# Weight splits of a transformer trunk: all high parts on ScalarE, fewer low parts on GpSimd

## The chip, the cores and the metric

The kernel runs on one core of a Trainium2 chip. The metric is device time in microseconds (us) of one execution, as the median of three runs. The engines of the core are TensorE (matmuls, PE in the profile, with its weight loads as PEld), VectorE (DVE), ScalarE (ACT), GpSimd (POOL) and SyncE (SP, which here issues most DMAs).

## The reference, cut to what matters

The program computes two layers (DEPTH = 2) of a diffusion trunk over 256 latent tokens and 256 context tokens of width 1024, in float32. Layer 0 works on both kinds of token (512 columns), layer 1 produces only the latent tokens (256 columns), though its keys and values also read the context. Each layer has two halves:

```python
m, mc = mixer_block(modulate(x, sh1, sc1), modulate(xc, sh1c, sc1c), with_ctx, ...)
x = layer_norm(ALPHA * x + g1 * m, ln1_g[l], ln1_b[l])
f = conv_ffn(modulate(x, sh2, sc2), ffn_w1[l], ffn_b1[l], ffn_conv_w[l], ffn_conv_b[l], ffn_w2[l], ffn_b2[l])
x = layer_norm(ALPHA * x + g2 * f, ln2_g[l], ln2_b[l])
```

The mixer has four branches on one input projection: a recurrent branch (a short convolution, gates, and a linear scan in both directions), differential attention, grouped-query attention with rotary embedding, and neighbourhood attention. The four results are multiplied by their branch weights, gated by `sigmoid` of 4096 further columns of the input projection, added, and projected. The feed-forward is

```python
u = dwconv(h @ w1 + b1, conv_w, conv_b, FFN_CONV // 2)
val, gate = jnp.split(u, 2, axis=-1)
return (jax.nn.silu(gate) * val) @ w2 + b2
```

with 2 x 2816 columns in `w1` and a depthwise convolution of three taps along the tokens.

## The kernel before, in words

Every large product is made from float32 operands split in two: a high part, which is the operand rounded to the type that TensorE takes at its faster rate, and a low part, the operand minus its high part. `mm3` (line 223) then adds three matmuls: high by high (line 225), and the two mixed products (lines 226 and 227). So each weight that arrives by DMA has to be split on the chip before it can be used.

Weights arrive in tiles of 1 MB named `raw` (two buffers; `raw`, line 160, issued on SyncE). Each holds two blocks of 128 x 1024 elements: a block is 128 columns of an input projection with its 8 slices of the contraction, or half of a token-major one, or a row of a second projection. `split` (line 188) turns one block into the tiles `wh` and `wl`, which are rings of four buffers each, so a block can be split while up to three earlier ones are waiting or in use. A few blocks go to tiles kept for longer (`wo`, and `w` for rows of the feed-forward's second projection), some in halves. `split` is reached from `cols_fm`, `cols_tm` and `rows`, and is called 271 times in one execution.

Which engine makes each part is decided by the running number of the split and the table `POOL` (line 105), by layer and phase. Phase 0 is the recurrent branch with its gates, 1 differential attention, 2 grouped-query attention, 3 neighbourhood attention with the merge and output projection, 4 the feed-forward with its second projection. An entry has four numbers: where the running number modulo the first is the second, GpSimd makes the high part, else ScalarE; where it is modulo the third the fourth, GpSimd makes the low part, else VectorE. The two decisions are independent, so that one block can have both parts on GpSimd.

The other work of these engines around the splits: in the feed-forward (`ffn`, line 1247), each block's result in PSUM is moved out by ScalarE twice (line 1268 into `up` with bias, line 1272 into `cv` scaled by the middle tap), VectorE adds the two outer taps (line 1275), ScalarE applies SiLU (line 1278), GpSimd multiplies the two halves (line 1279), and the product is split by ScalarE and VectorE (lines 804 and 805 in `hilo`). GpSimd also clears the border columns of `up` (lines 1266 and 1267). A pair of blocks of the value half and one of the gate half make one turn of the loop over `pair`, which has 11 turns in each layer. PSUM has three buffers for these results. In the recurrent branch (`lru`, line 686) VectorE runs the scans (lines 771 to 776) while TensorE works on the gate columns of that branch (`gates`, line 615). In attention, VectorE takes the row maxima (line 845) and ScalarE the exponentials (line 846).

The order of the instructions on each engine is not the order of the program text: `TileContext(nc, schedule_with_timeline_sim=True)` orders them at build time by a simulated timeline, within the program's data dependencies, a few hand-written ones (`hold`, `issue_after`) and the buffers of each tag. On the chip each engine then runs its list in that order.

Of the kernel before, what the change touches and what calls it, by code (L numbers as in the profile page):

```python
# [12 lines left out]
ALU = mybir.AluOpType  # L13
# [88 lines left out]

POOL = (((4, 0, 8, 2), (4, 0, 8, 2), (4, 0, 8, 0), (5, 2, 8, 2), (6, 5, 8, 2)), ((4, 0, 4, 1), (4, 0, 4, 2), (4, 0, 100, 6), (4, 0, 4, 2), (2, 0, 4, 0)))


LATE = ((8, 8, 4, 8), (8, 8, 4, 8))
# [2 lines left out]
class Trunk:  # L111
# [76 lines left out]
    def split(self, src, hi, lo):  # L188

        nc = self.nc  # L190
        self.n_split += 1
        ph, po, lp, lo_at = POOL[self.l][self.phase]
        if self.n_split % ph == po:
            nc.gpsimd.tensor_scalar(out=hi, in0=src, scalar1=1.0, scalar2=0.0, op0=ALU.mult, op1=ALU.add)  # L194
        else:
            nc.scalar.copy(hi, src)  # L196
        eng = nc.gpsimd if self.n_split % lp == lo_at else nc.vector
        eng.tensor_tensor(out=lo, in0=src, in1=hi.bitcast(F32), op=ALU.subtract)  # L198
        return hi, lo

# [1302 lines left out]
```

## Time and profile before

| | before |
|---|---|
| median of 3 runs | 1532.49 us (1530.24 to 1534.35) |
| profiled execution | 1532.55 us |
| its span | 1530.8 us |
| TensorE busy | 1421.7 us (93%) |
| TensorE weight loads busy | 1173.0 us (77%) |
| VectorE busy | 968.4 us (63%) |
| ScalarE busy | 640.8 us (42%) |
| GpSimd busy | 505.5 us (33%) |
| mean HBM traffic | 137 GB/s |

The span is the time from the first to the last recorded instruction; the execution's own time is a little longer. Shares of busy time are means over stages. The stages, in us from the start of the span: layer 0's mixer to about 500, its output stage to 560, its feed-forward to 818 and second projection to 935, layer 1's mixer from 960 to 1265, its output stage to 1318, its feed-forward to 1464, its second projection and the end to 1531. TensorE's matmuls are pipelined and their ends are modelled, so a busy TensorE is not necessarily at its peak; the starts of consecutive matmuls tell its rate.

### The profile page before, as it was taken

How to read it: one execution, taken by the hardware profiler on the slowest of the kernel's cores; microseconds unless marked ns; L12 is line 12 of the kernel's file. 1: busy time of each engine (PE TensorE's matmuls, PEld its weight loads, DVE VectorE, ACT ScalarE, POOL GpSimd, SP SyncE). 2: the span in 40 equal slices, each digit the busy share in tenths (PEclk: the TensorE clock that was granted, in tenths of full speed). 3: DMA queues.
4: the chain of work that ended last, by engine and by line, in shares of the span. 5: the costliest groups of instructions: out<-in, count | busy, mean ns of one | idle time of the engine just before them, and what ended most of it. 6: DMA issues, size and time to landing. Idle time of an engine off the chain costs nothing.

```text
span 1530.8 us, 22339 instructions
## 1 busy us (share of the span) xinstructions
PE 1421.7 (93%) x8420; PEld 1173.0 (77%) x8420; DVE 968.4 (63%) x1692; ACT 640.8 (42%) x1137; POOL 505.5 (33%) x612
## 2 busy tenths in 40 slices
PE   5989999899999989999999999988889997899987
PEld 3757767777877768777778887888688985798976
DVE  4674665743534987555554428775776558799965
ACT  3452353153254345444444124572525254455522
POOL 2241001421433523222222402250122545466662
PEclk9999999999999999999999999998899999899999
DMA  9336612223524354444444432434423546355562
GB/s 344 129 110 188 201 56 86 88 83 96 172 93 155 106 194 141 165 146 159 166 138 137 152 138 74 154 114 124 163 87 112 147 143 199 132 166 165 166 222 109
DMA packets 149022, 218.90 MB, mean 143 GB/s; under 512 B 9990, under 2 KB 118882, under 8 KB 148914
## 3 DMA queue, kind: packets, MB, share of 16 engines
q1 hardware_dynamic: 146402, 212.74, 42.0%
q0 software_dynamic: 2512, 4.73, 1.2%
q8 instruction: 67, 1.10, 0.3%
q14 instruction: 41, 0.34, 0.1%
HBM read 208.23 MB, written 1.08 MB: 137 GB/s over the span
## 4 chain that ended last, share of the span: by engine, by line
PE 65%; DVE 15%; issue 6%; DMA 5%; ACT 5%; POOL 2%; SPq 2%; DVEq 0%; ACTq 0%; POOLq 0%
PE mm L225 15%; PE mm L226 14%; PE mm L227 14%; DVE wl L198 4%; PE acc L227 3%; PE acc L226 3%; PE acc L225 3%; DVE cv L1275 3%; PE ops L869 3%; PE adaps L362 2%; ACT wh L196 2%; DMA raw<-in_w_in_dram 2%; PE tp L861 2%; DMA raw<-in_ffn_w_dram 1%; POOL cv L1279 1%
## 5 line engine op out<-in xcount | busy, mean ns | idle before, releaser
L225 PE MATMUL mm<-hh,wh 128*128 128x256 f32 (+1 forms) x1488 | 505.0, 342 | 17.9 <-POOL wh L194 5.3
L227 PE MATMUL mm<-hh,wl 128*128 128x256 f32 (+1 forms) x1488 | 498.7, 336 | 2.3 <-DVE wl L198 1.3
L226 PE MATMUL mm<-hl,wh 128*128 128x256 f32 (+1 forms) x1488 | 499.0, 336 | 0.5 <-DVE hl L344 0.5
L198 DVE TENSOR_TENSOR wl<-raw,wh 128x1024 fp32r<-128x1024 f32 x212 | 284.1, 1346 | 171.4 <-ACT wh L196 134.3
L225 PEld LDWEIGHTS mm<-hh,wh 128*128 128x128 f32 x1488 | 285.3, 193 | 63.9 <-issue 17.5
L196 ACT CAST wh<-raw 128x1024 fp32r<-128x1024 f32 x182 | 189.7, 1047 | 293.3 <-PE mm L226 110.0
L227 PEld LDWEIGHTS mm<-hh,wl 128*128 128x128 f32 x1488 | 285.1, 192 | 33.4 <-issue 2.5
L226 PEld LDWEIGHTS mm<-hl,wh 128*128 128x128 f32 x1488 | 285.4, 192 | 32.7 <-issue 4.0
L1275 DVE SCALAR_TENSOR_TENSOR cv<-up,par,cv 128x512 f32<-128x512 f32 (+1 forms) x176 | 157.9, 907 | 43.2 <-ACT cv L1272 30.9
L194 POOL TENSOR_SCALAR wh<-raw 128x1024 fp32r<-128x1024 f32 x73 | 89.5, 1226 | 270.4 <-PE mm L226 96.8
L198 POOL TENSOR_TENSOR wl<-raw,wh 128x1024 fp32r<-128x1024 f32 x43 | 116.3, 2706 | 117.2 <-ACT wh L196 104.9
L1279 POOL TENSOR_TENSOR cv<-cv 128x512 f32<-128x512 f32 (+1 forms) x44 | 54.2, 1232 | 155.5 <-ACT cv L1278 155.5
L226 PE MATMUL acc<-wl,a 128*128 128x512 f32 x232 | 92.3, 398 | 4.2 <-DVE wl L198 3.0
L227 PE MATMUL acc<-wh,a 128*128 128x512 f32 x232 | 92.0, 397 | 0.0
L225 PE MATMUL acc<-wh,a 128*128 128x512 f32 x232 | 91.1, 398 | 0.0
L845 DVE TENSOR_REDUCE nm<-sps 128x1 f32<-128x512 f32 (+1 forms) x96 | 56.3, 598 | 51.4 <-PE sps L890 34.6
L846 ACT ACTIVATE e<-sps,nm 128x512 f32<-128x512 f32 (+1 forms) x96 | 59.1, 618 | 64.1 <-DVE nm L845 50.5
L225 PE MATMUL mm<-wh,hh 128*128 128x256 f32 x240 | 68.6, 286 | 0.0
L227 PE MATMUL mm<-wh,hl 128*128 128x256 f32 x240 | 68.3, 284 | 0.0
L226 PE MATMUL mm<-wl,hh 128*128 128x256 f32 x240 | 67.8, 283 | 0.0
L293 ACT ACTIVATE junk<-x,nmu 128x512 bf16<-128x512 f32 x44 | 31.7, 721 | 85.3 <-DVE nmu L285 47.6
L1278 ACT ACTIVATE cv<-cv 128x512 f32<-128x512 f32 (+1 forms) x44 | 23.1, 525 | 94.1 <-DVE cv L1275 93.9
(311 smaller groups left out, 2323.6 us busy)
## 6 DMA issues: line engine op xcount, KB each, us to landing
raw<-in_ffn_w_dram SPq DMA_DIRECT2D x66, 1024.0 KB
raw<-in_w_in_dram SPq DMA_DIRECT2D x52, 1024.0 KB
raw<-in_w_ada_dram SPq DMA_DIRECT2D x40, 1024.0 KB
raw<-in_w_branch_dram SPq DMA_DIRECT2D x8, 1024.0 KB
raw<-in_w_out_dram SPq DMA_DIRECT2D x8, 1024.0 KB
w<-in_w_ada_dram SPq DMA_DIRECT2D x4, 1024.0 KB
w<-in_w_ada_dram SPq DMA_DIRECT2D x8, 512.0 KB
qk<-dp SPq DMA_DIRECT2D x48, 64.0 KB
```

What stands on the lines that cost most here:

```text
L194: nc.gpsimd.tensor_scalar(out=hi, in0=src, scalar1=1.0, scalar2=0.0, op0=ALU.mult, op1=ALU.add)
L196: nc.scalar.copy(hi, src)
L198: eng.tensor_tensor(out=lo, in0=src, in1=hi.bitcast(F32), op=ALU.subtract)
L225: nc.tensor.matmul(out, lhsT=lh, rhs=rh, start=start, stop=False)
L226: nc.tensor.matmul(out, lhsT=lh, rhs=rl, start=False, stop=False)
L227: return nc.tensor.matmul(out, lhsT=ll, rhs=rh, start=False, stop=stop)
L293: nc.scalar.activation(self.junk, halves[n], AF.Square, bias=nmu, accum_out=q[n])
L845: nc.vector.tensor_reduce(out=nm, in_=s if fold is None else fold, op=ALU.max, axis=AX.X, negate=True)
L846: nc.scalar.activation(e, s, AF.Exp, bias=nm, accum_out=total)
L869: self.last_pv = nc.tensor.matmul(o[64 * hh:64 * hh + 64, cs], lhsT=v[:, kt, vcol(hh)], rhs=pts[hh][:, kt, :], start=kt == 0, stop=kt == n ...
L1275: nc.vector.scalar_tensor_tensor(out=cv, in0=up[:, :, k:k + 256], scalar=tap[k], in1=cv, op0=ALU.mult, op1=ALU.add)
L1279: nc.gpsimd.tensor_tensor(out=conv[0], in0=conv[0], in1=conv[1], op=ALU.mult)
```

## The change

The table loses its rule for high parts, and `split` loses the branch: every high part is made by ScalarE. The rule for low parts stays as it was in phases 1 to 4 (an entry that never matched a split, in phase 2 of layer 1, is now `None`), and in phase 0 of both layers no low part is made by GpSimd. Nothing else is edited; the planner orders the new program anew.

```diff
-POOL = (((4, 0, 8, 2), (4, 0, 8, 2), (4, 0, 8, 0), (5, 2, 8, 2), (6, 5, 8, 2)), ((4, 0, 4, 1), (4, 0, 4, 2), (4, 0, 100, 6), (4, 0, 4, 2), (2, 0, 4, 0)))
+POOL = ((None, (8, 2), (8, 0), (8, 2), (8, 2)), (None, (4, 2), None, (4, 2), (4, 0)))
...
         nc = self.nc
         self.n_split += 1
-        ph, po, lp, lo_at = POOL[self.l][self.phase]
-        if self.n_split % ph == po:
-            nc.gpsimd.tensor_scalar(out=hi, in0=src, scalar1=1.0, scalar2=0.0, op0=ALU.mult, op1=ALU.add)
-        else:
-            nc.scalar.copy(hi, src)
-        eng = nc.gpsimd if self.n_split % lp == lo_at else nc.vector
+        nc.scalar.copy(hi, src)
+        turn = POOL[self.l][self.phase]
+        eng = nc.gpsimd if turn and self.n_split % turn[0] == turn[1] else nc.vector
         eng.tensor_tensor(out=lo, in0=src, in1=hi.bitcast(F32), op=ALU.subtract)
         return hi, lo
```

Counted through the program's order of splits (the counts of the page agree), by layer and phase:

| layer, phase | splits | high parts on GpSimd before | after | low parts on GpSimd before | after |
|---|---|---|---|---|---|
| 0, recurrent | 12 | 3 | 0 | 2 | 0 |
| 0, attention and merge (1 to 3) | 56 | 12 | 0 | 7 | 7 |
| 0, feed-forward and second projection | 69 | 12 | 0 | 8 | 8 |
| 1, recurrent | 14 | 3 | 0 | 3 | 0 |
| 1, attention and merge (1 to 3) | 54 | 14 | 0 | 9 | 9 |
| 1, feed-forward and second projection | 66 | 33 | 0 | 16 | 16 |
| all | 271 | 77 | 0 | 45 | 40 |

## Rows read from the trace of the kernel before

**Rows 1.** Page, costliest groups: line, engine, operation, tiles, count, then busy, mean ns, idle.
```profile
L196 ACT CAST wh<-raw 128x1024 fp32r<-128x1024 f32 x182 | 189.7, 1047 | 293.3 <-PE mm L226 110.0
...
L194 POOL TENSOR_SCALAR wh<-raw 128x1024 fp32r<-128x1024 f32 x73 | 89.5, 1226 | 270.4 <-PE mm L226 96.8
L198 POOL TENSOR_TENSOR wl<-raw,wh 128x1024 fp32r<-128x1024 f32 x43 | 116.3, 2706 | 117.2 <-ACT wh L196 104.9
```

**Rows 2.** Busy time by stretch; the last is one pair of blocks.
```profile
560.00:818.00 258.00, 254.87 (x1388) 201.36 (x1387) 150.38 (x232) 124.57 (x180) 68.09 (x148) 0.99 0.48 159
1035.00:1160.00 125.00, 109.39 (x763) 98.27 (x762) 88.63 (x194) 44.86 (x83) 22.54 (x21) 0.88 0.39 121
1160.00:1265.00 105.00, 101.02 (x788) 92.13 (x788) 55.34 (x87) 50.86 (x96) 47.37 (x49) 1.00 0.42 135
1318.00:1464.00 146.00, 138.85 (x1079) 133.42 (x1079) 133.85 (x143) 75.34 (x155) 92.23 (x141) 1.00 0.48 158
1361.60:1374.65 13.05, 12.16 (x99) 11.68 (x98) 12.18 (x13) 6.74 (x16) 8.56 (x13) 1.00 0.50 163
```

**Rows 3.** Groups of 1318 to 1464 us by form: busy, mean ns, idle before, releaser.
```profile
L1275 DVE SCALAR_TENSOR_TENSOR cv<-up,par,cv 128x256 f32<-128x256 f32 x88 | 85.6, 991 | 6.4 <-ACT cv L1272 4.8
...
L1278 ACT ACTIVATE cv<-cv 128x256 f32<-128x256 f32 x22 | 9.2, 418 | 49.9 <-DVE cv L1275 49.9
...
L194 POOL TENSOR_SCALAR wh<-raw 128x1024 fp32r<-128x1024 f32 x23 | 30.0, 1304 | 24.3 <-DMA raw<-in_ffn_w_dram 15.3 <-PE mm L226 8.1 <-PE mm L227 0.9
```

**Rows 4.** Two lines in that stretch: ns minimum/median/maximum, first and last start us.
```profile
L1275 DVE SCALAR_TENSOR_TENSOR cv<-up,par,cv x88: 471/954/2624, 1321.3 to 1463.0; 128x256 f32<-128x256 f32 x88
...
L198 DVE TENSOR_TENSOR wl<-raw,wh x34: 1209/1214/1978, 1321.7 to 1463.4; 128x1024 fp32r<-128x1024 f32 x34
```

**Rows 5.** Timeline, one pair of blocks: start us, us, engine, line, operation, idle before.
```profile
1362.39 1.05 POOL L194 TENSOR_SCALAR wh<-raw 128x1024 fp32r<-128x1024 f32 x1 [0.94 <-DMA raw<-in_ffn_w_dram]
...
1369.72 1.45 POOL L194 TENSOR_SCALAR wh<-raw 128x1024 fp32r<-128x1024 f32 x1 [0.41 <-PE mm L227]
...
1362.69 1.82 DVE L198 TENSOR_TENSOR wl<-raw,wh 128x1024 fp32r<-128x1024 f32 x1 [0.53 <-ACT wh L196]
...
1370.18 1.27 DVE L1275 SCALAR_TENSOR_TENSOR cv<-up,par,cv 128x256 f32<-128x256 f32 x1
...
1363.54 0.19 PEld L225 LDWEIGHTS mm<-hh,wh 128*128 128x128 f32 x1 [0.94 <-POOL up L1267]
...
1364.48 0.28 PE L226 MATMUL mm<-hl,wh 128*128 128x256 f32 x1
1364.60 0.28 PE L227 MATMUL mm<-hh,wl 128*128 128x256 f32 x1
```

**Rows 6.** Timeline of the recurrent branches: GpSimd low parts, and VectorE beside them.
```profile
985.80 2.50 POOL L198 TENSOR_TENSOR wl<-raw,wh 128x1024 fp32r<-128x1024 f32 x1 [1.96 <-ACT wh L196]
...
1003.39 2.41 POOL L198 TENSOR_TENSOR wl<-raw,wh 128x1024 fp32r<-128x1024 f32 x1 [0.24 <-ACT wh L196]
...
985.96 3.42 DVE L198 TENSOR_TENSOR wl<-raw,wh 128x1024 fp32r<-128x1024 f32 x1
...
1024.40 3.36 DVE L198 TENSOR_TENSOR wl<-raw,wh 128x1024 fp32r<-128x1024 f32 x1
```

**Rows 7.** Timeline around the longest TensorE wait for a GpSimd high part.
```profile
104.48 1.06 ACT L196 CAST wh<-raw 128x1024 fp32r<-128x1024 f32 x1 [3.17 <-DMA raw<-in_w_in_dram]
...
108.42 2.28 DVE L198 TENSOR_TENSOR wl<-raw,wh 128x1024 fp32r<-128x1024 f32 x1
...
109.59 2.02 POOL L194 TENSOR_SCALAR wh<-raw 128x1024 fp32r<-128x1024 f32 x1
...
111.66 0.80 PE L225 MATMUL mm<-hh,wh 128*128 128x512 f32 x1 [5.34 <-POOL wh L194]
...
112.68 0.63 PE L227 MATMUL mm<-hh,wl 128*128 128x512 f32 x1
113.11 0.63 PE L225 MATMUL mm<-hh,wh 128*128 128x512 f32 x1
```

## The prediction

> **What bounds the kernel now.** I read the page's table of engines first: TensorE is busy 93% of the span, VectorE 63%, ScalarE 42%, GpSimd 33%. Two thirds of the chain of waits is TensorE, so an edit to the weight splits is worth something only where TensorE stands still and waits for them. The second view is therefore busy time by stretch [rows 2]. In the feed-forward of layer 0 (560 to 818 us) TensorE is busy 254.87 of 258 us; nothing that happens to a split shows there. In the feed-forward of layer 1 (1318 to 1464 us), where half as many tokens pass each weight, TensorE is busy 138.85 of 146, VectorE 133.85, GpSimd 92.23 and ScalarE only 75.34. There the loop over pairs of blocks repeats every 13.05 us, with VectorE busy 12.18 of them, so VectorE sets the pace. TensorE's own need is less: consecutive 256-column matmuls start 0.12 us apart [rows 5], a pair has 4 blocks of 24, and 96 x 0.12 = 11.5 us. Its weight loads show the rest as gaps, such as the 0.94 us at 1363.54 [rows 5].
>
> The third view is durations. VectorE's convolution step takes 471 ns at best, 954 in the median and 2624 at worst, its low part 1209 at best and 1978 at worst [rows 4]. The same instruction on the same shape differs that much by what GpSimd does beside it: the low part at 1362.69 takes 1.82 us while GpSimd makes a high part from 1362.39 to 1363.44, and the convolution step at 1370.18 takes 1.27 us beside the GpSimd high part at 1369.72 [rows 5]. GpSimd pays as well: its high part has a mean of 1304 ns here [rows 3].
>
> **The change part by part.** The rules by remainder give 77 high parts on GpSimd before (the page shows 73 under one tile name [rows 1]; four go to kept tiles) and none after: 33 in layer 1's feed-forward and second projection (22 and 11), 12 in layer 0's, 26 in the mixers outside the recurrent branches with their output projections, 6 in the recurrent stretches (one of them at the start). Five of 45 low parts move from GpSimd to VectorE. The work itself costs ScalarE what it cost GpSimd: 1047 ns a cast [rows 1] against 1.05 us undisturbed [rows 5]. What matters is who waits.
>
> *Layer 1's feed-forward, 22 casts.* VectorE loses per pair 1.82 - 1.21 = 0.61 us to one GpSimd high part and 1.27 - 0.47 = 0.80 to the other [rows 4, 5], 1.41 together. Without them its 13.05 us become 11.64, just above TensorE's 11.5. Nothing can be gained beyond 13.05 - 11.5 = 1.55 a pair, 17 us over 11 pairs; nothing at all if VectorE then waits for ScalarE instead. ScalarE gets 2 x 1.05 = 2.1 us a pair on top of 6.74 busy [rows 2]: 8.8 of 11.6. Its largest idle piece is the wait of SiLU for the convolution, 49.9 us over the stretch or 4.5 a pair [rows 3], and a cast that the planner puts ahead of that wait costs nothing. That cover is the choice: the planner fills simulated idle time, and this is ScalarE's longest. If the cover is gone, up to 22 x 1.05 = 23 us stand on the path. I take 1.1 of the 1.41 per pair, because some VectorE relief will reappear as a wait for a cast: 11 x 1.1 = 12 us gained. Ends: 17 gained, 23 lost.
>
> The Trainium skill ("SBUF — State Buffer", Who interferes with whom) says that a VectorE instruction with two SBUF inputs and a GpSimd instruction that reads SBUF exclude each other: the second blocks until the first ends. The worst convolution step of 2624 ns fits it; by it every high part could block VectorE for its whole 1.05 us, and the pair would be TensorE-bound: the 17 us end. My 1.41 is the measured overlap, not the rule's maximum of 2.1.
>
> *Layer 1's second projection, 11 casts.* After its first blocks the chain there is matmuls one after another; splits run ahead. Zero, the same cover as in layer 0.
>
> *Layer 0's feed-forward and second projection, 12 casts.* ScalarE is busy 124.57 of 258 us [rows 2], blocks are split up to four ahead. Zero; if that cover failed, 12 x 1.05 = 13 us lost.
>
> *Mixers outside the recurrent branches, 26 casts.* ScalarE is idle half of the time or more there (44.86 of 125 us busy, 50.86 of 105 [rows 2]), but its exponentials stand on the attention's path. A cast in front of one delays it by up to 1.05, 27 us in all; the relief of VectorE's row maxima and low parts, at 0.61 to 0.80 a collision, is up to 16 to 21 us. Neither end is likely: most of these stretches is paced by projections. The two are of one size, and I take zero. Where both halves of a landed weight were cast side by side and are now cast in a row, VectorE's first low part (1.21 us) covers the second cast (1.05).
>
> *Low parts in the recurrent branches.* Each costs VectorE 1.21 us more. Against it stand the blocks they cause: at 985.96 a VectorE low part took 3.42 us beside the GpSimd one at 985.80, and at 1024.40 one took 3.36, so 2.2 and 2.15 us are given back; the GpSimd one at 1003.39 fell into VectorE's idle time and gives nothing [rows 6]. The one in layer 0 overlaps a scan, and I count it like the first two; the one at the start I count nothing for. Sum: 5 x 1.21 - 2.2 - 2.15 - 2.2 = -0.5 us of VectorE, zero in effect. Ends: 6 us lost (no relief) and 5 gained (each of the five relieved by 2.2).
>
> *One wait that goes.* TensorE stands 5.34 us before 111.66 and is released by a GpSimd high part that ran 109.59 to 111.61, behind GpSimd's last additions of the recurrent branch; ScalarE had cast the other block of that stretch at 104.48 [rows 7] and was then idle. After the gap matmuls start 0.43 us apart (112.68, 113.11 [rows 7]): that is about twice their usual spacing, the lower of TensorE's two clock levels, 1.2 GHz. Cast by ScalarE, this block is ready early. Next late is VectorE's low part at 108.42, which takes 2.28 us now and is itself stretched by that GpSimd cast [rows 7]: without it, it would end at 108.42 + 1.21 = 109.6 instead of the restart at 111.66. That is 2 us, and 1 more for the clock: 3 us gained. Ends: 0, and 5.34 plus some 2 us of slow matmuls = 7.
>
> Sum against the profiled execution (1532.55 us, span 1530.8, 1.75 around it; the median of the runs is 1532.49, the same): 1532.5 - 12 - 3 = 1517.5.
>
> **The rivals.**
> A, slower: ScalarE's one queue becomes the pace. Place: layer 1's feed-forward, between the cast of the finished activations and the evacuation of the next PSUM tile (lines 1268 and 1272), where TensorE already stands 0.94 us [rows 5]. If the planner puts both added casts there, the evacuation comes 2.1 us later in each pair; the relief of 1.41 does not cover it: 11 x 0.7 = 8 us lost. The same queue would then also delay the mixers' exponentials, by half a microsecond (an estimate: half a cast) at 26 casts, 13 us, of which relief gives back half: 6 more. With the 3 us above still gained, 1532.5 + 8 + 6 - 3 = 1543.5. It decides from the point where the evacuation is later than now by more than VectorE's 1.41. For it: the queue already waits in order. Against it: ScalarE's idle time is mostly elsewhere [rows 3]. The Trainium skill ("TensorE: Matmul & The Clock Gate", section "Architectural detail: the array is 16× 32×32, not 1× 128×128") says ScalarE's queue is strictly first in, first out, which is what would make this wait; the rows here show waits in order, and none by a cast alone.
>
> B, no change: VectorE's relief turns into waits for casts (it already idles 0.53 us before 1362.69 for one [rows 5]), and the wait at 111.66 is replaced by VectorE's recurrence: 1532.5 - 2 = 1530.
>
> C, larger: layer 1's feed-forward falls to TensorE's 11.5 us a pair (-17) and the 111.66 wait goes whole (-7): 1508.5.
>
> **How the numbers follow.** Forecast 0.50 (its own range 1511 to 1525), C 0.14, B 0.15, A 0.21. A difference below 0.3%, 4.6 us, can't be told from none. Forecast and C are faster, with a little of B: 0.66. B gives most of same: 0.14. A and its milder forms: 0.20. The range runs from below C's middle, 1503, to 1541, which takes in all of B and the smaller half of A; the unknown order of casts in the mixers is as wide as that.
>
> **What would show it.** Right: the pair period in layer 1's feed-forward at 11.6 to 12.2 us, the convolution step's mean well under its 991 ns [rows 3], its maximum still near 2.6 because one low part a pair stays on GpSimd; the 0.94 us gaps gone; no 5.34 us gap near 111; layer 0's feed-forward unchanged. Wrong: a period still at 13 with VectorE idle for ScalarE (B), TensorE's gaps before a block's first matmul grown to 2 us behind lines 1268 and 1272 (A), or a new wait of attention scores for exponentials of more than 10 us.

## The result and the profile after

The changed kernel takes 1505.83 us (median of 4 runs, 1500.30 to 1509.74); the kernel before, run beside it, 1532.01 (1530.24 to 1534.35). The ratio is 0.9823 with a 95% interval of 0.9800 to 0.9845; a repeat in another set of runs gave 0.9807 (0.9788 to 0.9826). The gain is 26 us. The forecast was 15: its direction and its range held, its size was too small.

Behind the edit the line numbers of the changed kernel are 3 lower (the cast's 4): the cast of a high part is L192, the low part L195, the matmuls L222 to L224, the convolution step L1272, SiLU L1275. The page of the changed kernel, busy time by engine and then two groups (line, operation, count, busy, mean ns, idle before):

```profile
PE 1410.1 (94%) x8420; PEld 1168.7 (78%) x8420; DVE 933.1 (62%) x1697; ACT 712.8 (47%) x1214; POOL 393.2 (26%) x530
...
L192 ACT CAST wh<-raw 128x1024 fp32r<-128x1024 f32 x255 | 264.5, 1048 | 344.6 <-PE mm L223 156.6
...
L195 POOL TENSOR_TENSOR wl<-raw,wh 128x1024 fp32r<-128x1024 f32 x38 | 93.9, 2471 | 203.7 <-ACT wh L192 165.6
```

Against [rows 1]: ScalarE has 255 casts of this shape where it had 182, at the same 1048 ns; GpSimd has no high part, and its 38 low parts take 2471 ns in place of 2706. ScalarE's queue of work grew and still fits. (The 38 are those of one tile name; with the two that go to kept tiles GpSimd makes 40.)

The stretches answer to [rows 2]; columns are start and end, length, then busy time (and count) of PE, PEld, DVE, ACT and POOL, the granted clock, the DMA share and GB/s. First layer 0's feed-forward, then 118.7 us of layer 1's, then one pair of blocks:

```profile
560.00:814.00 254.00, 249.05 (x1323) 197.14 (x1322) 143.34 (x216) 128.65 (x180) 60.42 (x141) 0.99 0.46 155
1316.00:1434.70 118.70, 118.70 (x991) 118.70 (x991) 100.70 (x136) 91.86 (x167) 47.79 (x112) 1.00 0.55 178
1343.81:1355.33 11.52, 11.52 (x99) 11.52 (x98) 9.79 (x13) 8.71 (x17) 4.54 (x12) 1.00 0.58 184
```

Layer 0 is much as it was. In layer 1 a pair takes 11.52 us, not 13.05, and TensorE is busy for all of it: the stretch went over from VectorE's pace to TensorE's own. VectorE now has 1.73 us of slack a pair.

The groups of that stretch (1312 to 1448 us), beside [rows 3]:

```profile
L1272 DVE SCALAR_TENSOR_TENSOR cv<-up,par,cv 128x256 f32<-128x256 f32 x88 | 64.8, 736 | 18.0 <-ACT cv L1269 15.6
L192 ACT CAST wh<-raw 128x1024 fp32r<-128x1024 f32 x46 | 48.2, 1049 | 32.9 <-PE mm L223 27.6 <-DMA raw<-in_ffn_w_dram 4.3 <-PE acc L224 0.7
...
L195 POOL TENSOR_TENSOR wl<-raw,wh 128x1024 fp32r<-128x1024 f32 x11 | 26.5, 2410 | 10.2 <-ACT wh L192 10.2
...
L1275 ACT ACTIVATE cv<-cv 128x256 f32<-128x256 f32 x22 | 9.1, 415 | 0.7 <-DVE cv L1272 0.7
```

The convolution step's mean fell from 991 to 736 ns, and SiLU's wait for it from 49.9 us to 0.7. What ScalarE idles now stands in front of the casts, 32.9 us, most of it until TensorE has released a block. Minimum, median and maximum in ns, beside [rows 4]:

```profile
L1272 DVE SCALAR_TENSOR_TENSOR cv<-up,par,cv x88: 469/480/1876, 1316.9 to 1440.5; 128x256 f32<-128x256 f32 x88
```

The median is now the undisturbed duration (480, before 954). The long ones that are left stand beside the one GpSimd low part of each pair, shorter delays beside GpSimd's product of the two halves. The timeline shows the former (start, us, engine, line, operation, idle before):

```profile
1342.96 2.41 POOL L195 TENSOR_TENSOR wl<-raw,wh 128x1024 fp32r<-128x1024 f32 x1 [0.78 <-ACT wh L192]
...
1343.81 2.71 DVE L1272 SCALAR_TENSOR_TENSOR cv<-up,par,cv 128x256 f32<-128x256 f32 x2 [1.43 <-ACT cv L1269]
1346.45 1.21 DVE L195 TENSOR_TENSOR wl<-raw,wh 128x1024 fp32r<-128x1024 f32 x1
...
1344.71 1.05 ACT L192 CAST wh<-raw 128x1024 fp32r<-128x1024 f32 x1 [0.69 <-PE mm L223]
1345.66 0.47 ACT L1265 ACTIVATE up<-mm,par 128x256 f32<-128x256 f32 x1
```

The cast at 1344.71 waits 0.69 us for TensorE to release its block, and the evacuation at 1345.66 follows at once behind it; TensorE does not stop for either.

**Where the 22.8 us between the two profiled spans (1530.8 and 1508.0) lie.** Stages are cut at the starts of TensorE's first and last matmul of each. By this cut the feed-forward of layer 1 ran from 1312.9 to 1454.0 us before; the 1318 to 1464 us of [rows 2] take in 10 us of the second projection. Two profiles of the changed kernel itself differ by 4.0 us in layer 0's feed-forward and by 5.6 in layer 1's mixer (363.9 and 358.3), so differences of that size say nothing in those stages; in the last two rows the two profiles agree within 0.7.

| stage | before | after |
|---|---|---|
| layer 0, start to the end of the mixer's projection | 544.8 | 539.6 |
| layer 0, feed-forward and second projection | 402.7 | 404.3 |
| layer 1, mixer up to the feed-forward's first matmul | 365.3 | 363.9 |
| layer 1, feed-forward, first to last matmul | 141.12 | 128.79 |
| layer 1, second projection, first to last matmul | 67.41 | 61.90 |

The feed-forward of layer 1 gives 12.3, its second projection 5.5, layer 0's mixer about 5. The second projection was forecast at zero. Its start shows where the time was: what TensorE waited for from 1454.1 to 1477.96 in the kernel before (what, us in total, times, longest),

```profile
PE acc L226 <- DVE wl L198: 3.0, 1, 3.0
PE acc L226 <- POOL wl L198: 1.2, 1, 1.2
```

and in the changed kernel at the same place of the program, 1436.7 to 1455.2:

```profile
PE acc L223 <- POOL wl L195: 0.5, 1, 0.5
```

The same two stretches, with columns as above, first before and then after:

```profile
1454.10:1477.96 23.86, 19.64 (x79) 15.21 (x77) 18.14 (x15) 9.34 (x16) 18.12 (x14) 0.93 0.68 220
...
1436.70:1455.20 18.50, 17.99 (x80) 14.30 (x78) 13.48 (x12) 8.99 (x13) 11.44 (x8) 1.00 0.77 249
```

In the kernel before the granted clock fell to 0.50, the lower level of 1.2 GHz, from 1471.9 to 1475.3 us, right behind the wait of 3.0 us; here it stayed at 1.00. The waits differ by 3.7 us and TensorE's busy time by 1.65: together they are the 5.4 by which the stretch is shorter.

### The profile page after: what moved, and what is told of

The parts are those of the page before. It is cut to its first block, busy times and chain, and to the rows that moved or that the text cites. A ratio compares the mean times of both kernels' runs of the same rounds, so it can differ in the third digit from the quotient of the medians.

```text
span 1508.0 us, 22307 instructions
## 1 busy us (share of the span) xinstructions
PE 1410.1 (94%) x8420; PEld 1168.7 (78%) x8420; DVE 933.1 (62%) x1697; ACT 712.8 (47%) x1214; POOL 393.2 (26%) x530
## 4 chain that ended last, share of the span: by engine, by line
PE 56%; DVE 7%; ACT 4%; DMA 3%; issue 3%; POOL 0%; SPq 0%; DVEq 0%; ACTq 0%
PE mm L222 13%; PE mm L223 13%; PE mm L224 13%; PE acc L223 4%; PE acc L224 4%; PE acc L222 4%; PE ops L866 2%; PE adaps L359 2%; DVE wl L195 1%; PE tp L858 1%; DMA raw<-in_w_in_dram 1%; ACT wh L192 1%; ACT junk L290 1%; DMA raw<-in_w_ada_dram 1%; DVE ml L802 1%
## 5 line engine op out<-in xcount | busy, mean ns | idle before, releaser
L222 PE MATMUL mm<-hh,wh 128*128 128x256 f32 (+1 forms) x1488 | 504.0, 342 | 13.0 <-ACT gate L625 8.1
L224 PE MATMUL mm<-hh,wl 128*128 128x256 f32 (+1 forms) x1488 | 498.7, 336 | 1.5 <-DVE wl L195 1.5
L192 ACT CAST wh<-raw 128x1024 fp32r<-128x1024 f32 x255 | 264.5, 1048 | 344.6 <-PE mm L223 156.6
L195 DVE TENSOR_TENSOR wl<-raw,wh 128x1024 fp32r<-128x1024 f32 x217 | 279.4, 1295 | 192.9 <-ACT wh L192 189.4
L222 PEld LDWEIGHTS mm<-hh,wh 128*128 128x128 f32 x1488 | 285.8, 193 | 55.4 <-issue 10.6
L224 PEld LDWEIGHTS mm<-hh,wl 128*128 128x128 f32 x1488 | 285.6, 192 | 33.7 <-issue 4.1
L1272 DVE SCALAR_TENSOR_TENSOR cv<-up,par,cv 128x512 f32<-128x512 f32 (+1 forms) x176 | 136.4, 775 | 53.5 <-ACT cv L1269 38.4
L195 POOL TENSOR_TENSOR wl<-raw,wh 128x1024 fp32r<-128x1024 f32 x38 | 93.9, 2471 | 203.7 <-ACT wh L192 165.6
L224 PE MATMUL acc<-wh,a 128*128 128x512 f32 x232 | 91.4, 395 | 0.0
L222 PE MATMUL acc<-wh,a 128*128 128x512 f32 x232 | 90.6, 395 | 0.0
L1276 POOL TENSOR_TENSOR cv<-cv 128x512 f32<-128x512 f32 (+1 forms) x44 | 49.6, 1128 | 152.6 <-ACT cv L1275 152.5
L222 PE MATMUL mm<-wh,hh 128*128 128x256 f32 x240 | 68.7, 286 | 0.0
L224 PE MATMUL mm<-wh,hl 128*128 128x256 f32 x240 | 68.0, 283 | 0.0
L1269 ACT ACTIVATE cv<-mm,cb,par 128x512 f32<-128x512 f32 (+1 forms) x88 | 58.5, 665 | 0.0
L359 PE MATMUL adaps<-raw,silu_c 128*32 128x256 f32 x640 | 47.8, 416 | 10.9 <-DMA raw<-in_w_ada_dram 8.8
```

The costliest lines, as they stand in the source:

```text
L222: nc.tensor.matmul(out, lhsT=lh, rhs=rh, start=start, stop=False)
L224: return nc.tensor.matmul(out, lhsT=ll, rhs=rh, start=False, stop=stop)
L359: nc.tensor.matmul(ps[32 * g:32 * g + 32, :], lhsT=self.silu_c[:, kk + k2, :], rhs=raw[:, k2, 256 * g:256 * g + 256], start=(k2 == 0), sto ...
L1269: nc.scalar.activation(cv, view(ps, 2, 256)[:, 0:nseg, :], AF.Identity, bias=self.cb[:, j:j + 1], scale=tap[1])
L1272: nc.vector.scalar_tensor_tensor(out=cv, in0=up[:, :, k:k + 256], scalar=tap[k], in1=cv, op0=ALU.mult, op1=ALU.add)
L1276: nc.gpsimd.tensor_tensor(out=conv[0], in0=conv[0], in1=conv[1], op=ALU.mult)
```

## The experiments

The theory after the result: GpSimd's high parts and VectorE get in each other's way, and this paced layer 1's feed-forward; the rest of the gain is elsewhere. Rivals: the gain is GpSimd's own time (it was too busy for its other work, whatever it read); it is the order in which blocks are handed over; it comes from the mixers. Ratios are to the kernel before, run beside each; "stretch" is layer 1's feed-forward from its first to its last matmul in the profile, 141.12 us before, 140.7 to 141.5 in the six profiles with GpSimd's high parts there and 128.8 to 129.7 in the six without them (and without idle instructions in their place).

**The high parts of layer 1's feed-forward and second projection alone.** On the kernel before; 999 is a period that never comes round.

```diff
 # POOL, layer 1, last entry
-(2, 0, 4, 0)
+(999, 998, 4, 0)
```

> The kernel before, with only the 33 high parts of layer 1's feed-forward and second projection moved to ScalarE. If the gain sits there, as the traces suggest (from the first feed-forward matmul of layer 1 to the first matmul of its second projection 141.1 us before, 128.8 after; the second projection 67.4 and 61.9), the time falls by 14 to 18 us to about 1516 and the stretch to 129 us. If the gain needs the other moves too (the planner's new order of the whole program), under 8 us.

1515.19 us, ratio 0.9874 (0.9839 to 0.9909), stretch 129.71, second projection 62.52. These 33 casts alone give 19 us of the 26; 11.4 and 4.9 of them are in the two stages named, the rest is not placed.

**The reverse: the changed kernel with that one step put back.**

```diff
-        nc.scalar.copy(hi, src)
+        if self.back and self.n_split % 2 == 0:   # back: layer 1's feed-forward only
+            nc.gpsimd.tensor_scalar(out=hi, in0=src, scalar1=1.0, scalar2=0.0, op0=ALU.mult, op1=ALU.add)
+        else:
+            nc.scalar.copy(hi, src)
```

> The changed kernel, with 22 high parts of layer 1's feed-forward blocks back on GpSimd (not those of the second projection). Contention theory: VectorE is blocked again, the stretch goes from 128.8 back to about 141 us and the time rises by some 12 us to about 1518. Rival (the gain came from the order of the rest): it rises by less than 4 us.

1525.17 us, 0.9945 (0.9927 to 0.9962); stretch 141.08, as before. The groups of the stretch (1312 to 1450 us):

```profile
L1277 DVE SCALAR_TENSOR_TENSOR cv<-up,par,cv 128x256 f32<-128x256 f32 x80 | 76.5, 975 | 6.3 <-ACT cv L1274 4.9
...
L194 POOL TENSOR_SCALAR wh<-raw 128x1024 fp32r<-128x1024 f32 x20 | 24.9, 1247 | 21.2 <-DMA raw<-in_ffn_w_dram 11.8 <-PE mm L227 8.6 <-PE mm L228 0.8
```

Both directions agree: the step is the cause, and a convolution step of 975 ns returns with it. The time rose by more than the 12 us expected: 19 to 21 by the ratios, of which 12.3 are in the stretch, 2.1 in the second projection (64.01 us, though its own casts stayed on ScalarE), and the rest is not placed. Neither direction excludes the rival of the order, since the planner orders each of these programs anew.

**What about a GpSimd instruction costs: its reads, or its time?** Two kernels keep the casts on ScalarE and add to the changed kernel, behind the cast of every second block of this feed-forward, one GpSimd instruction on a scratch tile that nothing else uses: a multiplication that reads and writes it, or a memset that only writes it.

```diff
-        nc.scalar.copy(hi, src)
+        cast = nc.scalar.copy(hi, src)
+        if self.back and self.n_split % 2 == 0:
+            self.after(nc.gpsimd.tensor_scalar(out=self.scr, in0=self.scr, scalar1=1.0, scalar2=0.0, op0=ALU.mult, op1=ALU.add), cast)
```

> The changed kernel, plus 22 GpSimd instructions of the old shape (tensor_scalar, 128x1024 float32, reading and writing a scratch tile) in layer 1's feed-forward, each behind the ScalarE cast of the block whose high part GpSimd made before. Nobody uses the scratch tile. Contention theory (GpSimd's reads block VectorE): VectorE's convolution steps slow down again, a loss of 5 to 13 us. Hand-over theory (what cost time was that others waited for GpSimd's high part): no loss, within 3 us.

```diff
+            self.after(nc.gpsimd.memset(self.scr, 0.0), cast)
```

> The same with 22 memsets of the same tile instead, which write and read nothing. If reads of SBUF are what blocks VectorE, as the Trainium skill (SBUF — State Buffer, Who interferes with whom) says for two-input VectorE instructions, there is no loss, within 3 us, and the convolution step's median stays at 480 ns. If GpSimd being occupied is what costs (its own products and border memsets come later), it loses what the reading twin loses.

With reads 1513.21 us, 0.9860 (0.9821 to 0.9899); with writes 1511.48, 0.9844 (0.9803 to 0.9886). Against the changed kernel's two ratios that is 6 to 8 us lost with reads and 3 to 6 with writes; the intervals of the two overlap. The stretches are further apart than repeats are: 135.21 and 131.89. The reads' groups (1312 to 1450 us in both):

```profile
L1276 DVE SCALAR_TENSOR_TENSOR cv<-up,par,cv 128x256 f32<-128x256 f32 x88 | 78.0, 887 | 8.4 <-ACT cv L1273 5.1
...
L195 POOL TENSOR_SCALAR scr<-scr 128x1024 f32<-128x1024 f32 x20 | 32.4, 1621 | 7.7 <-ACT wh L193 7.4
```

and the writes':

```profile
L1276 DVE SCALAR_TENSOR_TENSOR cv<-up,par,cv 128x256 f32<-128x256 f32 x88 | 73.6, 836 | 14.5 <-ACT cv L1273 11.1
...
L195 POOL MEMSET scr<- 128x1024 f32 x20 | 19.1, 954 | 10.8 <-ACT wh L193 10.7
```

The timeline of the reads shows the mutual exclusion by itself:

```profile
1359.75 2.11 POOL L195 TENSOR_SCALAR scr<-scr 128x1024 f32<-128x1024 f32 x1
...
1359.72 1.22 DVE L198 TENSOR_TENSOR wl<-raw,wh 128x1024 fp32r<-128x1024 f32 x1
1360.86 2.15 DVE L1276 SCALAR_TENSOR_TENSOR cv<-up,par,cv 128x256 f32<-128x256 f32 x2
```

VectorE's low part began 0.03 us earlier and ran undisturbed to 1360.94; GpSimd's instruction, 1.05 us when alone, took 2.11, so about the low part's length more, and ended at 1361.86; the two convolution steps (0.48 each alone) took 2.15, so the first waited until then. The memset beside the same low part:

```profile
1350.10 0.96 POOL L195 MEMSET scr<- 128x1024 f32 x1
...
1350.12 1.22 DVE L198 TENSOR_TENSOR wl<-raw,wh 128x1024 fp32r<-128x1024 f32 x1
```

Both run as if alone, and the three convolution steps that met nothing but a memset took 479 ns on the mean. So it is the reads that block; but an instruction that blocks nobody still cost 2 to 3 us in the stretch. It also moves what comes behind it: the convolution step's median stayed near 480 ns (484), but its mean rose to 836, because GpSimd's low part, now behind a memset, met nine steps for 2.7 us each (ten for 1.84 in the changed kernel). What TensorE's weight loads waited for from 1316 to 1445 us, by the list of waits, first in the kernel before:

```profile
PEld mm L225 <- POOL up L1267: 4.1, 5, 1.0
PEld mm L225 <- issue: 2.7, 3, 0.9
PEld mm L225 <- ACT cv L1272: 2.0, 6, 0.3
```

with the high parts put back,

```profile
PEld mm L226 <- POOL up L1269: 5.5, 6, 1.0
```

with the reads,

```profile
PEld mm L227 <- POOL wl L198: 5.6, 8, 1.1
```

and with the writes:

```profile
PEld mm L227 <- POOL wl L198: 2.6, 5, 0.9
```

The changed kernel has no such wait at all. With the idle instructions TensorE waits for GpSimd's low part, which stands in the queue behind them: 2.6 us where they only take time, 5.6 where they block and are blocked.

With the high parts the list names a tile `up`: two memsets of 0.10 us on GpSimd that write the margins of the tile into which ScalarE then evacuates PSUM. No matmul reads that tile, and the name does not hold. One such gap, which the list gives to no releaser ("issue"):

```profile
1401.57 1.05 POOL L194 TENSOR_SCALAR wh<-raw 128x1024 fp32r<-128x1024 f32 x1 [1.09 <-DMA raw<-in_ffn_w_dram]
1402.56 0.10 POOL L1266 MEMSET up<- 128x1 f32 x1
1402.59 0.10 POOL L1267 MEMSET up<- 128x1 f32 x1
...
1401.95 0.55 ACT L1272 ACTIVATE cv<-mm,cb,par 128x256 f32<-128x256 f32 x1
...
1402.57 0.19 PEld L225 LDWEIGHTS mm<-hh,wh 128*128 128x128 f32 x1 [0.80 <-issue]
```

TensorE goes on at 1402.57, before the high part and the memsets have ended, and 0.07 us after ScalarE's second evacuation of a PSUM tile. In all 14 waits ahead of a block's first weight load from 1316 us on, whatever the list names, it goes on 0.05 to 0.07 us after the end of that evacuation; the memsets end anywhere from 0.2 us before to 0.1 after, or run at another time. So the evacuation is what releases TensorE: 8.7 us in this feed-forward before, 8.9 with the high parts put back, none in the changed kernel or with the idle instructions. The evacuation is late because ScalarE works its list in order. For the gap before 1363.54 [rows 5]:

```profile
1359.67 1.59 POOL L1279 TENSOR_TENSOR cv<-cv 128x256 f32<-128x256 f32 x1 [0.74 <-ACT cv L1278]
...
1361.29 0.41 ACT L804 CAST a<-cv 128x256 fp32r<-128x256 f32 x1 [1.71 <-POOL cv L1279]
1361.60 1.05 ACT L196 CAST wh<-raw 128x1024 fp32r<-128x1024 f32 x1
...
1362.92 0.56 ACT L1272 ACTIVATE cv<-mm,cb,par 128x256 f32<-128x256 f32 x1
```

ScalarE stands 1.71 us for GpSimd's product, which had waited for SiLU and then took 1.59 us beside a VectorE low part; the evacuation follows behind the two casts.

By differences of single stretches, the 12 us are some 3 for GpSimd's time, 3.3 for its reads (135.21 - 131.89), and 5.9 (141.08 - 135.21) for what else a high part on GpSimd brings. What makes up these 5.9 is open. SiLU's wait for the convolution, in front of the evacuations, is 43.2 us with the high parts put back and 0.7 and 2.9 with the idle instructions, although the convolution steps beside the reads are nearly as slow (887 and 975 ns on the mean). That points to the planner's other order on ScalarE, which is argued and not shown: no run keeps the order and changes the engine alone.

**GpSimd without any low part in layer 1's feed-forward.** On the changed kernel, `(4, 0)` to `None` there.

> The changed kernel, with the 16 low parts of layer 1's feed-forward and second projection taken from GpSimd as well. The pair period there is already TensorE's own 11.5 us, so if TensorE bounds it there is no gain in the feed-forward (128.8 us stays within 1) and at most 2 us in the second projection. If VectorE's blocked time (its convolution step still reaches 1876 ns beside GpSimd's low part) still costs anything, 2 to 6 us faster. If VectorE becomes the bound with 11 more low parts, slower.

1507.58 us, 0.9835 (0.9819 to 0.9850); stretch 129.40. No gain: TensorE was already the bound, though the collisions with GpSimd's low parts were gone (the longest convolution step took 1055 ns).

**The low parts of the recurrent branches alone.** On the kernel before:

```diff
 # POOL, first entry of layer 0, then of layer 1
-(4, 0, 8, 2)
+(4, 0, 999, 998)
...
-(4, 0, 4, 1)
+(4, 0, 999, 998)
```

> The kernel before, with only the low parts of the recurrent branches (five) taken from GpSimd. The prediction's sum says VectorE gets about as much work as it loses in blocked time, so no change, within 5 us. Rival: VectorE paces the recurrence and every low part of 1.21 us is late, 4 to 6 us slower in the stretch from layer 1's first matmul to its first merge (95.6 us before, 100.0 in the changed kernel). Other rival: the wait of 5.3 us near 111 us goes with the low part alone, 3 us faster.

1525.55 us, 0.9946 (0.9929 to 0.9963): 8 us, where the forecast counted nothing. In its profile layer 0's mixer takes 541.6 us (544.8 before) and layer 1's 359.2 (365.3), the latter about what two profiles of one kernel differ by.

**The mixers' 32 high parts alone** (first two numbers of those entries to 999, 998, all four phases, both layers).

> The kernel before, with only the 32 high parts of the recurrent, attention and merge phases moved to ScalarE, the feed-forwards and all low parts as before. The prediction's sum: 3 us gained, from the wait near 111 us, the attention stretches unchanged within 3 us each. Rival (ScalarE's exponentials come later behind the casts): 5 to 15 us slower. The stage times of the changed kernel say about 4 gained in layer 0's mixer and 1 in layer 1's.

1531.8 us, 0.9986 (0.9972 to 1.0001), and the wait near 111 us [rows 7] is still there, now with another releaser (46 to 135 us):

```profile
PE mm L227 <- DVE wl L198: 4.7, 2, 3.6
```

So the GpSimd high part that released TensorE in [rows 7] was late, but not the cause.

**One low part moved: the tenth block of layer 0's recurrent branch.** On the kernel before:

```diff
-        eng = nc.gpsimd if self.n_split % lp == lo_at else nc.vector
+        eng = nc.gpsimd if self.n_split % lp == lo_at and self.n_split != 10 else nc.vector
```

> The kernel before, with one instruction moved: the low part of split 10 (the gate columns of layer 0's recurrent branch), GpSimd to VectorE. Theory: that low part stands in GpSimd's queue behind the branch's own products, ends at 99.61 us, and so holds the raw tile whose buffer the next weight load needs (issued at 99.64); moved, the load is issued near 95.6 and TensorE's wait of 5.3 us near 111 falls below 2, with the high part of split 12 still on GpSimd: 3 to 5 us faster. Rival (that wait is set by the GpSimd high part, as the prediction had it): the wait stays above 4 us, no change.

1529.05 us over 11 runs, 0.9971 (0.9957 to 0.9986): one instruction, 4.4 us (2 to 7 by the interval). The long wait is gone though GpSimd still makes its high part there (TensorE, 46 to 135 us):

```profile
PE mm L227 <- DVE wl L198: 1.9, 3, 1.2
```

The chain in the kernel before:

```profile
92.57 4.24 POOL L786 TENSOR_TENSOR ge<-ge,lru 128x512 f32<-128x512 f32 x2 [5.24 <-DVE ge L785]
96.77 2.84 POOL L198 TENSOR_TENSOR wl<-raw,wh 128x1024 fp32r<-128x1024 f32 x1
...
99.64 0.37 SPq L163 DMA_DIRECT2D raw<-in_w_in_dram  x1
```

and what the DMA queue waited for there (80 to 112 us):

```profile
SPq L163 <- POOL wl L198: 5.6, 1, 5.6
```

The low part is the last reader of the landed weight `raw`, and it queues behind two products of the recurrence. Until it ends at 99.61 the buffer is taken (there are two), and the next weight's load is issued only at 99.64. With the high parts on ScalarE but this low part left, the queue has the same line, word for word. With the one low part moved that line is gone and the load starts 4 us earlier:

```profile
95.71 0.37 SPq L163 DMA_DIRECT2D raw<-in_w_in_dram  x1
...
102.44 1.49 POOL L194 TENSOR_SCALAR wh<-raw 128x1024 fp32r<-128x1024 f32 x1
```

The high part that came at 109.59 in [rows 7] now runs at 102.44. The granted clock of 0.50 that followed the wait (111.66 to 115.00 us) is gone with it: from 46 to 135 us the clock stays at 1.00. Layer 0's mixer takes 543.6 to 546.0 us in the four profiles with this low part on GpSimd and 539.1 to 542.7 in the eight with it on VectorE and the other low parts of that mixer as before. A third `raw` buffer, which would take the hold away in another manner, was not tried.

**Layer 1's three recurrent low parts alone** (`(4, 0, 4, 1)` to `(4, 0, 999, 998)`, the kernel before).

> The kernel before, with only the three low parts of layer 1's recurrent branch moved to VectorE. If the gain of the five together (0.54%, 8 us) is shared, 3 to 5 us faster here; if it all sits in layer 0, no change.

1531.24 us over 12 runs, 0.9990 (0.9976 to 1.0005): no difference that can be told. With the single one above this is 0.39%, where all five gave 0.54 (0.37 to 0.71). Whether the rest is the fifth, at the start, or chance is open.

**The changed kernel again, with no low part on GpSimd in the mixers, and with none at all.**

> The changed kernel itself, beside the others on the same chip: a ratio to before of 0.982, as first measured, within 0.003.

> The changed kernel, with the 16 low parts of the attention and merge phases of both layers taken from GpSimd too (the feed-forwards keep theirs). If holding raw tiles and blocking VectorE cost there what they cost in the recurrent branches (1.6 us a low part), up to 10 us faster than the changed kernel, a ratio near 0.975; if these stretches are paced by matmuls and exponentials, the same as it, 0.981.

> The changed kernel with no part of any split on GpSimd. Expected from the others: as the run without them in the attention phases, since layer 0's feed-forward has no wait to lose and layer 1's is at TensorE's own rate without them as with them: 0.975 to 0.983. If VectorE becomes the bound in layer 1's feed-forward, above 0.985.

In the second all four mixer entries of both layers are `None`, in the third every entry. Again: 1503.49 us, 0.9807 (0.9788 to 0.9826). Without mixer low parts: 1502.19, 0.9795 (0.9780 to 0.9810). None at all: 1501.87, 0.9803 (0.9782 to 0.9823). The three intervals overlap: no version here is shown to beat the changed kernel, and GpSimd's remaining 40 low parts make no difference that these times can tell. Layer 0's mixer did take only 534.5 and 534.7 us in the profiles of the last two, some 4.5 less than the shortest with its low parts on GpSimd; whether that is a gain is open.

## Why the prediction was right in direction and short in size

**Layer 1's feed-forward, 12 us: the size came out, the mechanism in part.** 12.3 in the profile. Without the high parts on GpSimd the stretch goes at TensorE's pace, as the step said, and no wait for a cast appeared, so the part that I kept back for such waits was not needed. The sum came out all the same because I had read a period off one pair and multiplied it by 11. From first matmul to first matmul the pairs took 14.25, 11.52 and 11.85 us, then seven times 12.9 to 13.2, and 12.2 for the last; in the changed kernel 13.7, nine times 11.52 and 11.4. So seven pairs gave about 1.5 us each, the last 0.8, and the first three 0.9 together. That two errors cancelled is luck.

ScalarE's cover, the choice in that step, held: SiLU's 49.9 us of waiting are gone, and no cast keeps TensorE waiting. The cost was read too narrowly. I priced VectorE's overlaps with the high parts at 1.41 us a pair; VectorE's busy time from the first to the last matmul of the stretch fell by 2.0 a pair (127.85 to 105.53 us). The longest steps of [rows 4], 2.6 us, stand beside GpSimd's low part, so they say nothing of what a high part blocks; even these fell to 1.84, though the low part stayed, and the sign that the maximum would remain near 2.6 did not come. And reads alone are some 3 of the 12 us; the rest is GpSimd's time and the open 5.9. That the gap before 1363.54 [rows 5] ends with ScalarE's evacuation, as rival A said, is right, though the list of waits names a memset.

The Trainium skill ("SBUF — State Buffer", Who interferes with whom) says that a VectorE instruction with two SBUF inputs and a GpSimd instruction that reads SBUF exclude each other. The runs agree: 2.11 and 2.15 us with reads, 0.96 and 1.22 beside a memset. By that rule the forecast was the 17 us end for this stretch, and its reason held: the stretch became TensorE-bound. Only the 17 was too much, for four of the eleven pairs had little to give.

**Second projection, 0: wrong.** The step said "splits run ahead". They did not at its start: TensorE stood 3.0 and 1.2 us for the first low parts, 0.5 after, and then had the lower clock for 3.4 us. I had looked at busy shares of the feed-forward and not at the waits of the stage behind it. VectorE brings a backlog into it: its last convolution step of the feed-forward ended 9.4 us after the second projection's first matmul, 4.2 us after it in the changed kernel, and the low parts come behind that. Measured 5.5 in the profile, 4.9 with the 33 casts alone; with the feed-forward's 22 put back, 2.1 of it returned, so that more than half goes with the projection's own 11 (by single profiles: 61.1 to 62.5 us with both on ScalarE, 67.2 to 69.0 with both as before).

**Layer 0's feed-forward and the mixers' high parts, 0: right.** The stretch of layer 0 shows no change; no run moved its 12 casts alone. The mixers' high parts alone gave 2 us with an interval that touches none. The single changes sum to 1.26 + 0.54 + 0.14 = 1.94%, the whole change measured 1.77 and 1.93; so nothing is left over for those 12 casts, within the 6 us or so that the intervals leave.

**Recurrent low parts, 0, and the wait near 111 us, 3: the sum was short by 5 and the cause was wrong.** I set 5 x 1.21 us of VectorE against its blocks and stopped there. The five give 8 us, and one of them 4.4. What I missed is the buffer: the low part reads `raw` last, so moving it frees a DMA buffer and starts a load 4 us earlier. In [rows 7] I followed the wait one step back, to the high part that released TensorE, and not on to why that one was late. The right rows were the DMA queue's waits, which I had not read. Taken alone, the high parts gave nothing there; the low part took the wait away, and the slow matmuls behind it.

**The rivals.** A: no sign in the feed-forward of the changed kernel, where evacuations follow casts without a TensorE wait. Over the whole span these are the waits of TensorE for a cast and for exponentials that the changed kernel's list of waits names at 1 us or more:

```profile
PE sps L997 <- ACT e L843: 3.4, 6, 1.4
...
PE sps L886 <- ACT e L843: 3.2, 3, 2.7
...
PE mm L222 <- ACT wh L192: 2.0, 1, 2.0
...
PE acc L222 <- ACT wh L192: 1.2, 1, 1.2
```

That is nearly 10 us in all; before, the two for exponentials were 4.5 and 1.0 and there was none of 1 us for a cast of ScalarE. The wait for the gates, ScalarE's too, rose from 4.8 to 8.4 (6.7 in the second profile of the changed kernel). So TensorE may have waited some 6 to 8 us more for ScalarE in the mixers, not the added 14 that A asked for, and the mixers' high parts moved alone lost nothing. B: excluded by the pair period. C, 1508.5, came nearest in time, but by other terms: 12.3 rather than 17 in the feed-forward, and the rest from two steps that I had at nothing.

## What to carry to other kernels

An instruction on an idle engine is not free: price what it blocks while it reads, what stands behind it in its queue (here the low parts that TensorE waited for 2.6 us behind memsets that blocked nobody), and which buffer it holds as the last reader. When a wait is released by a late instruction, ask what made that one late, down to the DMA queue's own waits, before crediting an edit with it. A releaser that a list of waits names is inferred: compare its end with the restart over many occurrences, as the evacuation's constant 0.05 to 0.07 us and the memsets' scatter did here. And when a stage is paced by an engine, look at the first waits of the next stage too: the backlog is paid there.

## What was not expected of the hardware

VectorE and GpSimd took turns: an instruction that takes 1.05 us alone took 2.11 beside a low part of 1.22, and of the next two VectorE steps the first, 0.48 alone, took 1.27 and ended 0.27 after it, although GpSimd's tile was one that VectorE never touches. A GpSimd memset of the same tile ran in 0.96 us beside the same low part at 1.22: it is the reading, and not the sharing of data, that excludes.
